# Sixteen-tile Strassen in the head phases, with most new sample states made later

## The chip, the cores and the metric

The kernel runs on one core of one Trainium2 chip. The metric is the device time of one execution in microseconds (us). Before the change it is 2170.14 us, the median of three runs (2167.53 to 2170.44).

## The reference

One inference step of a two-layer decoder trunk, in float32. A prompt group of 512 tokens and a sample group of 8 tokens share all weights, so the kernel works on 520 columns. Cut to what matters:

```python
def trunk_layer(x, p_i, pos, conv_buf, ret_S, norm_g, w_in, conv_w, gn_g, w_out, w_pg, w_ple):
    h = rmsnorm(x, norm_g)
    z = h @ w_in                                   # 2048 -> 8192
    b_c, c_c, x_c, g_c, q, k, v, g_r = split_projection(z)
    conv_y, new_buf = short_conv(c_c * x_c, conv_buf, conv_w)
    y_conv = b_c * conv_y * jax.nn.silu(g_c)
    q = rope(q...); k = rope(k...) * (RET_HEAD_DIM ** -0.5)
    o, new_S = retention(q, k, v, ret_S, retention_log_gamma())
    o = groupnorm(o, per head)
    y_ret = (o * gn_g) * jax.nn.silu(g_r)
    x = x + jnp.concatenate([y_conv, y_ret], axis=-1) @ w_out
    x = x + jax.nn.sigmoid(x @ w_pg) * (p_i @ w_ple)
    return x, new_buf, new_S
```

For a sample token the retention of one head (256 x 256 state S, 4 heads, 8 sample rows, so 32 states per layer) is S_new = gamma S + k v and o = q . S_new, which is also gamma (q . S) + (q . k) v. The new states are an output of the step, and o goes on into the group norm.

## The kernel before, in words

Activations lie transposed: 16 K tiles of 128 features by 520 columns. Every float32 product is made of three matmuls (`mm3`, L245 to L249): operands and weights are split into a high part, written by ACT, and the rest, written by DVE (`split_w`, L229 and L230, for weights; `split`, L551 and L552, for activations).

The projections run in pairs of 128-row output tiles (`pair`). A pair is computed plainly (`plain`) or with its first s K tiles by Strassen's scheme (`strassen`): two rows, two halves of the columns (260 each) and two halves of the K tiles form a 2 x 2 block product of seven products instead of eight. The rest of the K tiles, `chunks(s, KT)`, is done plainly into the same banks, with one more bank, `c`. Weight sums are made by DVE in `add` (L319) in place in the raw ring of 32 tiles; bank copies and sums are L307 and L312. Operand sums (`operand_sums`, L413 to L416) are made once per operand set and split. The number of Strassen tiles per pair stands in tables: `HEADS` and `CONVS` for the input projection, `OUT_ROWS` and `GATES` for the two others.

A layer has these phases. Heads: 16 pairs, four for each retention head (q, k, v, gate), and the prompt's retention in nine steps per head, popped aside of later pairs. Convolution: 8 steps j of two pairs. Then the output projection `wo` (8 pairs), and the gate projection `wg` with the embeddings (8 pairs, in the last layer 7 and an ending of its own). Each phase builds the operand set of the next as room allows (`Operands.fill`, with a reserve).

All buffers for activations are 75 slots of 520 columns, handed out first in, first out (`Slots`); split weights go through a ring of 60 tiles. Weight loads are issued by SP. Everything else, loads and stores of slots, goes through POOL's queue (`SIDE`). A simulated time line orders each engine's instructions by program order as priority; operations passed to `keep` stay in program order among themselves.

Sample states: `sample` is called from `head` (three times per two pairs) and from the convolution steps. It loads a state (`sample_load`: L770, and key and query of that row broadcast to all partitions, L771), and one call later runs `sample_step`: ACT scales the state by gamma (L776), DVE adds k v in two operations (L780), POOL stores the new state (L781), and two reductions (L784) make q . S_new into `osum`. After the last one `sample_norm` (L1371 to L1389) normalises all rows, beside the last convolution step.

Of the kernel before, what the change touches and what calls it, by code (L numbers as in the profile page):

```python
# [7 lines left out]
F32 = mybir.dt.float32  # L8
# [5 lines left out]
P = 128  # L14
D = 2048
KT = D // P
# [10 lines left out]
PLE = 256  # L27
PAST = 4096
EPS = 1e-6
NSLOT = 75  # L30
CH = 4
CHS = 4
CHA = 4
# [28 lines left out]
RAW = 32  # L62
WARM = 8
FIRST = 8
SPLIT = 60


def F(ap):
# [11 lines left out]
class Slots:  # L80
# [111 lines left out]
def trunk_kernel(  # L192
# [365 lines left out]
        return op  # L558


    vec = const.tile([P, 160], F32, name="vec")

    def norm_g(l, k):
        return vec[:, 16 * l + k : 16 * l + k + 1]
# [12 lines left out]
        c = 112 + 4 * h + m  # L577
        return vec[:, c : c + 1]

    def gam(h):  # L580
        return vec[:, 128 + h : 129 + h]
# [6 lines left out]
    scv = const.tile([P, CJ, 2, NS], F32, name="scv")  # L588
    vs = const.tile([P, H, 2, NS], F32, name="vs")
    osum = const.tile([P, 2, H, NS], F32, name="osum")  # L590
    gs = const.tile([P, 2 * H, NS], F32, name="gs")
    decay = const.tile([P, H, 3], F32, name="decay")

    G.memset(ones, 1.0)
    G.memset(onesd, 1.0 / HD)
    G.memset(half_neg, -0.5)

    yc = dram.tile([DEPTH, CJ, P, T], F32, name="yc")
    x1s = dram.tile([DEPTH, KT, P, T], F32, name="x1s")
# [75 lines left out]
    for a, b in ((0, 1), (1, 4), (4, 8), (8, 12), (12, 16)):  # L675
        raws = []
        if b == 1:
            raw = raw_ring.get(4)
            DMA.dma_start(raw.rearrange("p (m n) -> p m n", n=P), wi[0, 0:4, :, :P].rearrange("m p n -> p m n"))
            S.dma_start(vec, vecs)  # L680
            x = get()
            for n in (LEFT, RIGHT):
                DMA.dma_start(x[:, n], xT[0, :, n])
            xs.append(x)
            w = split_w(raw)
            ws = [[t[:, P * m : P * m + P] for t in w] for m in range(4)]
        else:
            for i in range(4):
                raws.append(load(wi[0, i, :, P * a : P * b]))
                if i < b - a:  # L690
                    x = get()
                    DMA.dma_start(x, xT[a + i])
                    xs.append(x)
            ws = [split_w(raw) for raw in raws]
            raw_ring.put(*raws)
        for k in range(a, b):
            X.ops[k] = split(xs[k], norm_g(0, k), free_src=False, halves=k % 2 == 0 and k < max(X.rows))
            for m in range(4):
                for h, n in enumerate((LEFT, RIGHT)):
                    product(first[m][h], ws[m], k - a, at(X.ops, [k], n), k == 0, k == KT - 1)  # L700
        if b == 1:
            raw_ring.put(raw)
            split_ring.put(*w)
            DMA.dma_start(ident, ident_d)
        else:
            for w in ws:
                split_ring.put(*w)
# [8 lines left out]
    for l in range(DEPTH):  # L716
# [49 lines left out]
            return g  # L766

        def sample_load(h, b):
            st, kb = get(), get()
            SIDE.dma_start(st[:, :512], sret[l, h, b])  # L770
            SIDE.dma_start(kb[:, :512], kq[l, h, b].rearrange("c d -> (c d)").partition_broadcast(P))  # L771
            return h, b, st, kb

        def sample_step(h, b, st, kb):

            keep(S.activation(st[:, :512], st[:, :512], AF.Identity, scale=gam(h)))  # L776
            k = kb[:, 256:512]
            for e in range(2):
                c = slice(256 * e, 256 * e + 256)
                keep(V.scalar_tensor_tensor(st[:, c], k, vs[:, h, e, b : b + 1], st[:, c], MUL, ADD))  # L780
            SIDE.dma_start(o_rets[l, h, b], st[:, :512])  # L781
            for e in range(2):
                c = slice(256 * e, 256 * e + 256)
                V.tensor_tensor_reduce(k, st[:, c], kb[:, :256], 1.0, 0.0, MUL, ADD, osum[:, e, h, b : b + 1])  # L784
            put(st, kb)

        loaded = []

        def sample():

# [2 lines left out]
            if todo:  # L793
                loaded.append(sample_load(*todo.pop(0)))

        todo = []

        res = xT if l == 0 else x2s[l - 1]
# [18 lines left out]
        def retain(h):  # L817
# [28 lines left out]
            vf = []  # L846
            for e, z in enumerate(head(mt + 4)):
                t = z.slot if z.ps is None else copied(z.ps).slot
                V.scalar_tensor_tensor(vs[:, h, e, :], t[:, SEQ:T], 1.0 / 16, rb[:, SEQ:T], MUL, MUL)
# [227 lines left out]
        for j in range(CJ):  # L1077
            mt = 32 + 4 * j
            O.ready = min(j // 2, 3)
            middle.append(sample)  # L1080
            zc, zx = pair(X, wi[l], mt, mt // 2 - skipped, O)
            u = get()
            times(u, zc, r2)
# [17 lines left out]
            if j == CJ - 1:  # L1101
                while loaded or todo:
                    sample()
                O.ready = 7
                sample_norm(nc, small, pr, osum, onesd, half_neg, gs, lambda k: gn_g(l, k))
            zg, zb = pair(X, wi[l], mt + 2, mt // 2 + 1 - skipped, O)
            gt = silu(zg)
            V.tensor_tensor(t, t, gt, MUL)
            put(gt)
# [20 lines left out]
        for m in range(0, KT, 2):  # L1130
            xs = [get(), get()]
            for i in range(2):
                SIDE.dma_start(xs[i], res[m + i])
            Gt.ready = m // 2
            middle.append(lambda: O.fill(MORE_OUT, 0))
            zs = pair(O, wo[l], m, m // 2, Gt)
            for i, (x, z) in enumerate(zip(xs, zs)):
# [37 lines left out]
        for m in range(0, KT - tail, 2):  # L1175
            pes, xs = [], [again(x1s, m), again(x1s, m + 1)]
            later.append(lambda m=m, w=parts(wp[l, m // 2], 0, 4), pes=pes: embed(m, w, pes))
            if X:
                X.ready = m // 2
            middle.append(lambda: Gt.fill(MORE_GATE, 0))  # L1180
            if tail and m == KT - tail - 2:
# [33 lines left out]
        if tail:  # L1215
# [141 lines left out]
                    DMA.dma_start(o_ys, few)  # L1357

            block_out(1)
        if l < DEPTH - 1:  # L1360
            X.ready = KT // 2


def sample_norm(nc, small, pr, osum, onesd, half_neg, gs, gn):

    V, G, PE = nc.vector, nc.gpsimd, nc.tensor
    n = H * NS
    flat = osum.rearrange("p e h b -> p e (h b)")
    ps = pr.tile([P, 512], F32, tag="r", name="ps_sm")
    for e in range(2):  # L1370
        PE.matmul(ps[:, :n], onesd, flat[:, e], start=e == 0, stop=e == 1)  # L1371
# [107 lines left out]
```

## Time and profile before

| | before |
|---|---|
| time of three runs, us | 2167.53, 2170.14, 2170.44 |
| span of the profiled execution, us | 2167.3 |
| DMA, mean | 179 GB/s, 387.31 MB |
| matmul records | 17861 |

The span goes from the first to the last instruction of one execution on the core; a run's time holds the span and what lies around it. The profiled execution is one, its own run time isn't listed. PE is TensorE, DVE VectorE, ACT ScalarE, POOL GpSimd, SP the engine that issues the weight loads. PEld is the loading of matmul weights, which overlaps PE. Busy times of PE are modelled, since matmuls are pipelined. In the groups of instructions, the columns are: line, engine, operation, output<-inputs, output shape<-input shape, count, then busy us and mean ns of one, then the idle time of the engine just before them and what released it.

### The profile page before, as it was taken

The page shows a single profiled execution, that of the slowest core. Times are in us where ns is not written, and L with a number is a line of the kernel's source. Part 1 is how long each engine was busy: PE and PEld are TensorE (multiplying, and loading weights), DVE is VectorE, ACT ScalarE, POOL GpSimd, SP SyncE. Part 2 cuts the span into 40 slices and gives each one's busy share as a digit, 9 for nine tenths or more (in the row PEclk, how much of TensorE's full clock was granted, in tenths as well). Part 3 has the DMA queues.
Part 4 walks back from the last instruction along what each step waited for, and adds up shares of the span by engine and source line. Part 5 has one row for each costly group of instructions (what it writes and reads, how often), then busy time and mean ns, then how long its engine had stood idle before and what let it go on. Part 6 is the DMA issues. An engine that isn't in the chain of part 4 may idle for free. (4 is left out here: it accounts for less than half of the span.)

```text
span 2167.3 us, 48178 instructions
## 1 busy us (share of the span) xinstructions
PE 2147.8 (99%) x17861; PEld 2142.1 (99%) x17861; DVE 1896.1 (87%) x3849; ACT 1264.5 (58%) x2647; POOL 430.6 (20%) x746
## 2 busy tenths in 40 slices
PE   9999999999999999999999999999999999999998
PEld 9999999999999999999999999999999999999998
DVE  8889988998999987987997988989999998879884
ACT  8656655565555655655765655565645555456565
POOL 2313222211001211200212222231111022011011
PEclk9999999999999999999999999999999999999999
DMA  8555565545543745645645566664464355566455
GB/s 288 171 175 197 181 217 184 178 157 175 158 129 118 238 156 187 215 154 160 215 144 175 172 213 191 189 209 170 151 182 149 120 158 202 176 207 200 128 164 198
DMA packets 182861, 387.31 MB, mean 179 GB/s; under 512 B 25888, under 2 KB 56352, under 8 KB 182624
## 3 DMA queue, kind: packets, MB, share of 16 engines
q1 hardware_dynamic: 128704, 212.98, 31.6%
q0 software_dynamic: 53056, 169.84, 23.8%
q8 instruction: 140, 2.29, 0.4%
q10 hardware_dynamic: 864, 1.39, 0.2%
q14 instruction: 97, 0.79, 0.1%
HBM read 318.96 MB, written 65.15 MB: 177 GB/s over the span
## 5 line engine op out<-in xcount | busy, mean ns | idle before, releaser
L247 PE MATMUL ps_g<-slot,split 128*128 128x260 f32 x5465 | 1531.6, 284 | 7.2 <-ACT slot L307 2.9
L248 PE MATMUL ps_g<-slot,split 128*128 128x260 f32 x5465 | 1534.3, 282 | 0.3 <-DVE slot L555 0.3
L249 PE MATMUL ps_g<-slot,split 128*128 128x260 f32 x5461 | 1519.9, 283 | 0.5 <-DVE split L230 0.5
L229 ACT ACTIVATE split<-raw 128x512 fp32r<-128x512 f32 (+2 forms) x1347 | 777.3, 596 | 583.1 <-DVE raw L319 213.2
L247 PEld LDWEIGHTS ps_g<-slot,split 128*128 128x128 f32 x5465 | 1024.0, 188 | 10.1 <-ACT slot L307 3.7
L248 PEld LDWEIGHTS ps_g<-slot,split 128*128 128x128 f32 x5465 | 1028.5, 188 | 0.5 <-DVE slot L555 0.5
L249 PEld LDWEIGHTS ps_g<-slot,split 128*128 128x128 f32 x5461 | 1019.8, 188 | 1.0 <-DVE split L230 1.0
L230 DVE TENSOR_TENSOR split<-raw,split 128x512 fp32r<-128x512 f32 (+2 forms) x1346 | 849.2, 652 | 172.5 <-PE ps_g L248 85.4
L319 DVE TENSOR_TENSOR raw<-raw 128x512 f32<-128x512 f32 (+1 forms) x660 | 428.9, 660 | 32.5 <-DMA raw<-wi 23.7
L307 ACT ACTIVATE slot<-ps_g 128x260 f32<-128x260 f32 x336 | 127.4, 381 | 140.6 <-PE ps_g L249 122.7
L551 ACT ACTIVATE slot<-slot 128x520 fp32r<-128x520 f32 (+1 forms) x212 | 109.2, 562 | 46.6 <-DVE slot L414 11.1
L552 DVE TENSOR_TENSOR slot<-slot,slot 128x520 fp32r<-128x520 f32 (+1 forms) x212 | 124.4, 620 | 4.1 <-ACT slot L551 3.9
L781 POOL DMA_DIRECT2D o_rets<-slot x64 | 35.3, 552 | 351.6 <-DVE slot L780 131.7
L307 DVE TENSOR_TENSOR slot<-ps_g,slot 128x260 f32<-128x260 f32 x168 | 70.9, 424 | 6.0 <-PE ps_g L249 3.7
L869 POOL DMA_DIRECT2D slot<-hs x64 | 46.2, 724 | 118.7 <-DVE split L230 42.7
L814 POOL DMA_DIRECT2D hs<-slot x64 | 35.6, 556 | 139.3 <-DVE slot L755 61.3
L780 DVE SCALAR_TENSOR_TENSOR slot<-slot,vs,slot 128x256 f32<-128x256 f32 x128 | 56.1, 481 | 4.5 <-ACT slot L776 4.3
L746 DVE TENSOR_TENSOR slot<-slot,slot 128x520 f32<-128x520 f32 x80 | 55.8, 698 | 4.7 <-DMA o_rets<-slot 3.7
L770 POOL DMA_DIRECT2D slot<-sret x64 | 35.5, 554 | 114.6 <-ACT split L229 37.3
L1058 POOL DMA_DIRECT2D slot<-x1s x76 | 40.8, 538 | 87.6 <-PE ps_g L249 27.2
L1209 POOL DMA_DIRECT2D x2s<-slot x30 | 16.4, 545 | 201.6 <-DVE slot L1204 200.6
L771 POOL DMA_DIRECT2D slot<-kq x64 | 34.9, 547 | 106.0 <-DVE slot L876 22.2
(217 smaller groups left out, 1733.8 us busy)
## 6 DMA issues: line engine op xcount, KB each, us to landing
raw<-wi SPq DMA_DIRECT2D x377, 256.0 KB, 3.9
raw<-wo SPq DMA_DIRECT2D x128, 256.0 KB, 5.4
raw<-wg SPq DMA_DIRECT2D x122, 256.0 KB, 4.1
raw<-wi SPq DMA_DIRECT2D x136, 192.0 KB, 4.0
slot<-x1s POOLq DMA_DIRECT2D x76, 260.0 KB, 5.1
slot<-sret POOLq DMA_DIRECT2D x64, 256.0 KB, 4.0
hs<-slot POOLq DMA_DIRECT2D x64, 256.0 KB, 4.0
slot<-hs POOLq DMA_DIRECT2D x64, 256.0 KB, 5.2
```

Source lines behind the costliest of these rows:

```text
L229: S.activation(hi, raw, AF.Copy)
L230: V.tensor_tensor(lo, raw, F(hi), SUB)
L247: PE.matmul(out, wh, xh, start=start, stop=False, skip_group_check=more)
L248: PE.matmul(out, wh, xl, start=False, stop=False, skip_group_check=more)
L249: PE.matmul(out, wl, xh, start=False, stop=stop, skip_group_check=more)
L307: fn(*args)
L319: V.tensor_tensor(out[:, n], x[:, n], y[:, n], op)
L551: keep(S.activation(hi, src[:, n], AF.Copy))
L552: V.tensor_tensor(lo, src[:, n], F(hi), SUB)
L746: V.tensor_tensor(out[:, n], v, table[:, n], MUL)
L780: keep(V.scalar_tensor_tensor(st[:, c], k, vs[:, h, e, b : b + 1], st[:, c], MUL, ADD))
L869: SIDE.dma_start(t[:, :512].rearrange("p (m n) -> p m n", m=2), src)
```

## The change

Head pairs that had 14 Strassen tiles get 16; so do the first two convolution pairs of each layer. The slots go from 75 to 76, the split ring from 60 to 56 tiles, and the table `vec` from 160 to 128 columns, since gamma becomes a constant of the instruction.

For 24 of the 32 sample states of a layer (rows b below 6) the new state is no longer made in `sample_step`. Only gamma (q . S) is reduced there, from the old state; the queries of two rows share a slot. The term (q . k) v is added in `sample_norm`, from products `qk` summed over the partitions by two matmuls with ones. The new states are made later by `update`, three calls deep: load the key, multiply it by v / gamma (two ACT operations), add the old state by an accumulating load from DRAM, and a call later scale by gamma and store. `update` is called three times per convolution step from the fourth on, once per pair in the output phase (m = 2 to 12) and in the gate phase (m = 2 to 10).

```diff
-NSLOT = 75
+NSLOT = 76
-HEADS = [[0, 0, 0, 8] + [14] * 12, [0] + [14] * 15]
-CONVS = [[14] * 2 + [16] * 13 + [14]] * 2
+GAMMA = [1.0 - 2.0 ** (-5 - h) for h in range(H)]
+HEADS = [[0, 0, 0, 8] + [16] * 12, [0] + [16] * 15]
+CONVS = [[16] * 15 + [14]] * 2
-SPLIT = 60
+SPLIT = 56
+LATE_STATES = 6
+UPDATES = 3
...
         def sample_load(h, b):
-            st, kb = get(), get()
+            st = get()
             SIDE.dma_start(st[:, :512], sret[l, h, b])
-            SIDE.dma_start(kb[:, :512], kq[l, h, b].rearrange("c d -> (c d)").partition_broadcast(P))
-            return h, b, st, kb
+            if b >= LATE_STATES:
+                kb = get()
+                SIDE.dma_start(kb[:, :512], kq[l, h, b].rearrange("c d -> (c d)").partition_broadcast(P))
+                return h, b, st, kb
+            if b % 2 == 0:
+                n = min(2, LATE_STATES - b)
+                queries.append(get())
+                src = kq[l, h, b : b + n, :2].rearrange("b c d -> b (c d)").partition_broadcast(P)
+                SIDE.dma_start(queries[-1][:, : 256 * n].rearrange("p (b c) -> p b c", b=n), src)
+            return h, b, st, queries[-1]
...
         def sample_step(h, b, st, kb):
...
+            for e in range(2):
+                c = slice(256 * e, 256 * e + 256)
+                n = slice(256 * (b % 2), 256 * (b % 2) + 256)
+                keep(V.tensor_tensor_reduce(st[:, c], st[:, c], kb[:, n], GAMMA[h], 0.0, MUL, ADD, osum[:, e, h, b : b + 1]))
+            put(st)
+            if b % 2 or b == LATE_STATES - 1:
+                put(kb)
...
+        def key_load(h, b):
+            st = get()
+            SIDE.dma_start(st[:, 256:512], kq[l, h, b, 2:].rearrange("c d -> (c d)").partition_broadcast(P))
+            return h, b, st
+
+        def state_add(h, b, st):
+            for e in range(2):
+                c = slice(256 * e, 256 * e + 256)
+                keep(S.activation(st[:, c], st[:, 256:512], AF.Copy, scale=vs[:, h, e, b : b + 1]))
+            SIDE.dma_start(st[:, :512], sret[l, h, b], accum_op=ADD)
+            return h, b, st
+
+        def state_out(h, b, st):
+            keep(S.activation(st[:, :512], st[:, :512], AF.Copy, scale=GAMMA[h]))
+            SIDE.dma_start(o_rets[l, h, b], st[:, :512])
+            put(st)
+
+        keyed, added = [], []
+
+        def update():
+            if added:
+                state_out(*added.pop(0))
+            if keyed:
+                added.append(state_add(*keyed.pop(0)))
+            if states:
+                keyed.append(key_load(*states.pop(0)))
+
+        states = [(h, b) for b in range(LATE_STATES) for h in range(H)]
...
+            some = slice(0, LATE_STATES)
+            V.scalar_tensor_tensor(qk[:, :, h, some], qks[:, :2, some], GAMMA[h], qks[:, 2:, some], MUL, MUL)
...
-                V.scalar_tensor_tensor(vs[:, h, e, :], t[:, SEQ:T], 1.0 / 16, rb[:, SEQ:T], MUL, MUL)
+                V.scalar_tensor_tensor(vs[:, h, e, :], t[:, SEQ:T], 1.0 / 16 / GAMMA[h], rb[:, SEQ:T], MUL, MUL)
+                rest = slice(SEQ + LATE_STATES, T)
+                V.scalar_tensor_tensor(vn[:, h, e, :], t[:, rest], 1.0 / 16, rb[:, rest], MUL, MUL)
...
             middle.append(sample)
+            if j >= UPDATES:
+                middle.append(update)
...
             zg, zb = pair(X, wi[l], mt + 2, mt // 2 + 1 - skipped, O)
+            if j >= UPDATES:
+                update()
...
             middle.append(lambda: O.fill(MORE_OUT, 0))
+            if 0 < m < KT - 2:
+                middle.append(update)
             zs = pair(O, wo[l], m, m // 2, Gt)
...
             middle.append(lambda: Gt.fill(MORE_GATE, 0))
+            if 0 < m < KT - 4:
+                middle.append(update)
...
+    ps = pr.tile([P, 512], F32, tag="r", name="ps_qk")
+    for d in range(2):
+        PE.matmul(ps[:, :n], ones, qk[:, d].rearrange("p h b -> p (h b)"), start=d == 0, stop=d == 1)
+    own = small.tile([P, 2, H, NS], F32, tag="sq", name="own", bufs=1)
+    for e in range(2):
+        V.tensor_tensor(own[:, e], vs[:, :, e], ps[:, :n].rearrange("p (h b) -> p h b", b=NS), MUL)
+        V.tensor_tensor(osum[:, e], osum[:, e], own[:, e], ADD)
     ps = pr.tile([P, 512], F32, tag="r", name="ps_sm")
```

The parts left out are the eight early rows of `sample_step` (as before, with gamma as a constant and `vn` for the values), the second `update` of a convolution step ahead of its second pair, and the declarations of `qk`, `vn` and `own`.

More of the change, by code (lines that the diff above doesn't have):

```diff
@@ L558, in split @@
         return op
-    vec = const.tile([P, 160], F32, name="vec")
+    vec = const.tile([P, P], F32, name="vec")
     def norm_g(l, k):
@@ L590, in trunk_kernel @@
     osum = const.tile([P, 2, H, NS], F32, name="osum")
+    qk = const.tile([P, 2, H, NS], F32, name="qk")
+    vn = const.tile([P, H, 2, NS - LATE_STATES], F32, name="vn")
     gs = const.tile([P, 2 * H, NS], F32, name="gs")
@@ L679, in trunk_kernel @@
             DMA.dma_start(raw.rearrange("p (m n) -> p m n", n=P), wi[0, 0:4, :, :P].rearrange("m p n -> p m n"))
-            S.dma_start(vec, vecs)
+            S.dma_start(vec, vecs[:, :P])
             x = get()
@@ new lines, in sample_load @@
+            if b % 2 == 0:
[4 more added lines that the diff above has]
+            return h, b, st, queries[-1]
+        def sample_step(h, b, st, kb):
+            if b >= LATE_STATES:
+                keep(S.activation(st[:, :512], st[:, :512], AF.Copy, scale=GAMMA[h]))
+                k = kb[:, 256:512]
+                for e in range(2):
+                    c = slice(256 * e, 256 * e + 256)
+                    v = vn[:, h, e, b - LATE_STATES : b - LATE_STATES + 1]
+                    keep(V.scalar_tensor_tensor(st[:, c], k, v, st[:, c], MUL, ADD))
+                SIDE.dma_start(o_rets[l, h, b], st[:, :512])
+                for e in range(2):
+                    c = slice(256 * e, 256 * e + 256)
+                    V.tensor_tensor_reduce(k, st[:, c], kb[:, :256], 1.0, 0.0, MUL, ADD, osum[:, e, h, b : b + 1])
+                put(st, kb)
+                return
@@ L778, in sample_step @@
             for e in range(2):
                 c = slice(256 * e, 256 * e + 256)
[L780 to L787, printed above, removed]
+                n = slice(256 * (b % 2), 256 * (b % 2) + 256)
@@ L794, in sample @@
                 loaded.append(sample_load(*todo.pop(0)))
+        def key_load(h, b):
[4 more added lines that the diff above has]
+            for e in range(2):
+                c = slice(256 * e, 256 * e + 256)
+                keep(S.activation(st[:, c], st[:, 256:512], AF.Copy, scale=vs[:, h, e, b : b + 1]))
+            SIDE.dma_start(st[:, :512], sret[l, h, b], accum_op=ADD)
+            return h, b, st
+        def state_out(h, b, st):
+            keep(S.activation(st[:, :512], st[:, :512], AF.Copy, scale=GAMMA[h]))
+            SIDE.dma_start(o_rets[l, h, b], st[:, :512])
+            put(st)
[8 more added lines that the diff above has]
+        states = [(h, b) for b in range(LATE_STATES) for h in range(H)]
         todo = []
@@ L1104, in trunk_kernel @@
                 O.ready = 7
-                sample_norm(nc, small, pr, osum, onesd, half_neg, gs, lambda k: gn_g(l, k))
+                sample_norm(nc, small, pr, osum, qk, vs, ones, onesd, half_neg, gs, lambda k: gn_g(l, k))
+            if j >= UPDATES:
+                middle.append(update)
             zg, zb = pair(X, wi[l], mt + 2, mt // 2 + 1 - skipped, O)
+            if j >= UPDATES:
+                update()
             gt = silu(zg)
@@ L1359, in trunk_kernel, with sample_norm @@
             block_out(1)
+        assert not (todo or loaded or states or keyed or added)
         if l < DEPTH - 1:
             X.ready = KT // 2
-def sample_norm(nc, small, pr, osum, onesd, half_neg, gs, gn):
+def sample_norm(nc, small, pr, osum, qk, vs, ones, onesd, half_neg, gs, gn):
     V, G, PE = nc.vector, nc.gpsimd, nc.tensor
@@ L1368, in sample_norm @@
     flat = osum.rearrange("p e h b -> p e (h b)")
+    ps = pr.tile([P, 512], F32, tag="r", name="ps_qk")
+    for d in range(2):
+        PE.matmul(ps[:, :n], ones, qk[:, d].rearrange("p h b -> p (h b)"), start=d == 0, stop=d == 1)
+    own = small.tile([P, 2, H, NS], F32, tag="sq", name="own", bufs=1)
+    for e in range(2):
+        V.tensor_tensor(own[:, e], vs[:, :, e], ps[:, :n].rearrange("p (h b) -> p h b", b=NS), MUL)
+        V.tensor_tensor(osum[:, e], osum[:, e], own[:, e], ADD)
     ps = pr.tile([P, 512], F32, tag="r", name="ps_sm")
```

10 lines of the change are left out of this document (6 added, 4 removed).

## The prediction

> **What bounds the kernel now.** I read the head of the page first (busy time by engine, then the 40 slices), after it the table of stages, the matmul groups with shapes kept apart, and the waits of PE.
>
> ```profile
> span 2167.3 us, 48178 instructions
> ...
> PE 2147.8 (99%) x17861; PEld 2142.1 (99%) x17861; DVE 1896.1 (87%) x3849; ACT 1264.5 (58%) x2647; POOL 430.6 (20%) x746
> ...
> PEclk9999999999999999999999999999999999999999
> ```
>
> ```profile
> core 0: us, PE busy (x) PEld busy (x) DVE busy (x) ACT busy (x) POOL busy (x), PEclk, DMA share, GB/s
> 0.00:100.00 100.00, 97.24 (x777) 95.85 (x778) 83.20 (x162) 70.23 (x140) 29.99 (x61) 1.00 0.68 231
> 100.00:600.00 500.00, 499.06 (x4170) 498.81 (x4169) 453.44 (x969) 291.59 (x627) 112.58 (x193) 1.00 0.57 180
> 600.00:800.00 200.00, 196.68 (x1636) 196.05 (x1635) 180.82 (x356) 112.97 (x244) 32.70 (x51) 1.00 0.53 164
> 800.00:1000.00 200.00, 200.00 (x1671) 200.00 (x1670) 169.38 (x314) 112.11 (x215) 30.10 (x56) 1.00 0.56 179
> 1000.00:1600.00 600.00, 598.93 (x5000) 597.74 (x4999) 534.97 (x1140) 362.64 (x775) 140.78 (x239) 1.00 0.58 183
> 1600.00:1800.00 200.00, 197.72 (x1640) 196.46 (x1639) 185.46 (x371) 113.30 (x244) 26.32 (x39) 1.00 0.50 156
> ...
> 2000.00:2167.30 167.30, 158.17 (x1313) 157.22 (x1311) 119.37 (x234) 92.14 (x197) 22.71 (x41) 0.99 0.50 163
> ```
>
> ```profile
> L247 PE MATMUL ps_g<-slot,split 128*128 128x260 f32 x5437 | 1523.6, 284 | 7.2 <-ACT slot L307 2.9 <-ACT ps_g L307 1.6 <-ACT split L229 1.5
> ```
>
> PE sets the time, at the full granted clock: it is idle for 2167.3 - 2147.8 = 19.5 us. By the table, 2.8 of these lie in the first 100 us, 9.1 in the last 167, 3.3 + 2.3 in the two stretches where the convolution phase hands over to the output projection (600:800 and 1600:1800), and 0.9 + 1.1 in all the rest. A matmul's mean of 284 ns is its pipelined length; its price is the distance between starts. In 800:1000, where PE never waits, 1671 starts fill 200 us: **0.1197 us each**. Nearly all of them are the 260-column matmuls, so a matmul taken away is worth 0.12 us as long as weights, operands and bank copies still come in time.
>
> **What the change removes.** A pair of output tiles costs 16 x 2 x 2 x 3 = 192 matmuls when plain. With s K tiles by Strassen it costs 7 x (s/2) x 3 plus (16 - s) x 4 x 3, which is 192 - 1.5 s: 171 for s = 14 and 168 for s = 16. From 14 to 16 go 12 head pairs of layer 0, 15 of layer 1, and two convolution pairs in each layer (the last one stays at 14): 31 pairs, 93 matmuls. **93 x 0.1197 = 11.1 us less on PE.**
>
> **What it adds on PE.** sample_norm gets two more matmuls of 32 columns per layer, beside two of that shape:
>
> ```profile
> 664.56 0.28 PE L249 MATMUL ps_g<-slot,split 128*128 128x260 f32 x1
> 664.68 0.53 PE L1371 MATMUL ps_sm<-osum,onesd 128*128 128x32 f32 x4
> 665.04 0.36 PE L247 MATMUL ps_g<-slot,split 128*128 128x260 f32 x1
> 665.24 0.28 PE L248 MATMUL ps_g<-slot,split 128*128 128x260 f32 x1
> ```
>
> The two of before hold the stream up by 665.24 - 664.68 - 0.12 = 0.44 us. Two more in two layers: **+0.9 us**. The four small DVE operations behind them (the nearest row is L849's 165 ns, below) delay the sample gates by under 1 us; those feed operands of the next phase and no matmul at once, so I put nothing down.
>
> **What a 16-tile pair costs the others.** DVE stands at 453.44 / 500 = 91% in the heads, so it must not grow.
>
> ```profile
> L230 DVE TENSOR_TENSOR split<-raw,split 128x512 fp32r<-128x512 f32 x1031 | 695.0, 690 | 147.8 <-PE ps_g L248 81.2 <-ACT split L229 51.8 <-issue 6.1
> L319 DVE TENSOR_TENSOR raw<-raw 128x512 f32<-128x512 f32 x520 | 354.1, 688 | 17.6 <-DMA raw<-wi 12.1 <-DMA raw<-wo 2.9
> L230 DVE TENSOR_TENSOR split<-raw,split 128x384 fp32r<-128x384 f32 x249 | 137.1, 555 | 16.2 <-ACT split L229 9.9 <-PE ps_g L248 3.4 <-ACT slot L551 1.9
> ...
> L319 DVE TENSOR_TENSOR raw<-raw 128x384 f32<-128x384 f32 x140 | 77.4, 554 | 14.9 <-DMA raw<-wi 11.6 <-DMA raw<-wg 2.8
> ...
> L780 DVE SCALAR_TENSOR_TENSOR slot<-slot,vs,slot 128x256 f32<-128x256 f32 x128 | 56.1, 481 | 4.5 <-ACT slot L776 4.3
> ...
> L230 DVE TENSOR_TENSOR split<-raw,split 128x256 fp32r<-128x256 f32 x66 | 27.3, 423 | 8.5 <-ACT split L229 7.6 <-PE ps_g L248 0.8
> ...
> L849 DVE SCALAR_TENSOR_TENSOR vs<-slot,slot 128x8 f32<-128x8 f32 x16 | 2.5, 165 | 0.1
> ```
>
> Splits per pair: 14 of 512 columns (9.66 us) for 7 of 512, 7 of 384 and 2 of 256 (9.56 us). The four weight sums grow by 4 x (688 - 554) ns = 0.54 us. Together +0.64 us. Against it, each late state drops its two L780 operations, 0.96 us. The heads take about 1.5 samples per pair and three in four are late: -1.08 us. New values and the q.k products add some 0.14 us per pair (L849's 165 ns twice and one like it, per head of four pairs). Net -0.3 us per 20 us pair: DVE keeps its margin. The price of that cover being gone: DVE at 18.2 us of work per 20 us pair has 1.8 us to spare, so +0.64 us without relief, as in the first head, is still hidden. SP issues 8 weight loads per pair where it issued 10, of the same bytes; the raw ring of 32 tiles is then full with four matrices of 8, as it is now in 13 convolution pairs per layer and in all 16-tile output pairs, which run at 200.00 of 200.
>
> The split ring loses 4 of 60 tiles: 7 chunks in flight instead of 7.5, that is 7 x 12 x 0.12 = 10 us of lead. PE does not feel half a chunk as long as ACT is the one that waits:
>
> ```profile
> ACT split L229 <- PE ps_g L249: 186.2, 220, 3.9
> ```
>
> It does, 220 times. I cost it at nothing; a hiccup of over 10 us would be needed.
>
> **Operands.** A 16-tile pair needs the eighth operand sum at once. Does it exist by then?
>
> ```profile
> L416 DVE TENSOR_TENSOR slot<-slot,slot x8: 421/430/435, 41.3 to 95.5; 128x260 f32<-128x260 f32 x8
> ```
>
> ```profile
> 1103.21 0.43 DVE L416 TENSOR_TENSOR slot<-slot,slot 128x260 f32<-128x260 f32 x1
> ...
> 1114.41 0.70 DVE L552 TENSOR_TENSOR slot<-slot,slot 128x520 fp32r<-128x520 f32 x1
> ```
>
> In layer 0 all eight sums (one L416 each) are made by 95.5 us, and the first pair concerned starts after 384 + 192 + 180 = 756 matmuls, near 93 us: free. In layer 1 the eighth is summed at 1103.2 and its splits run to 1115, in a stretch where DVE has little spare. One split of 0.70 us becomes due earlier. Bounds: nothing (other work moves back) and 3.1 us (a whole sum: four operations of 0.43 and two splits of 0.70). I take **+0.7 us**.
>
> **Late states.** Each late state keeps its two reductions, and moves elsewhere: a key load, two ACT copies of 256 columns, an accumulating load of the old state, one ACT copy of 512, the store.
>
> ```profile
> L229 ACT ACTIVATE split<-raw 128x512 fp32r<-128x512 f32 x1032 | 632.3, 626 | 462.3 <-DVE raw L319 188.2 <-PE ps_g L249 166.4 <-PE ps_g L248 45.1
> ...
> L776 ACT ACTIVATE slot<-slot,vec 128x512 f32<-128x512 f32 x64 | 45.7, 714 | 0.0
> ...
> L917 ACT ACTIVATE slot<-ps_kt,vec 128x256 fp32r<-128x256 f32 x32 | 15.0, 468 | 9.2 <-DMA hs<-slot 3.2 <-DVE slot L918 2.5 <-PE ps_kt L913 2.2
> ```
>
> ```profile
> L770 POOL DMA_DIRECT2D slot<-sret x64: 537/544/585, 50.5 to 1670.9; - x64
> ```
>
> ```profile
> slot<-sret POOLq DMA_DIRECT2D x64, 256.0 KB, 4.0
> ...
> slot<-kq POOLq DMA_DIRECT2D x64, 256.0 KB, 4.8
> o_rets<-slot POOLq DMA_DIRECT2D x64, 256.0 KB, 3.1
> ```
>
> ACT: 2 x 0.47 + 0.63 - 0.71 = +0.86 us per late state, at most three states per 40 us in the convolution phase and one per 20 us later, on an engine busy 55 to 60% there. POOL: 4.5 DMA issues for 3, so 48 x 1.5 x 0.54 = 39 us on an engine at 20%. Bytes: a second read of 48 x 256 KB = 12.6 MB. None of it feeds a matmul: **0** on PE, if nothing queues behind a wait. Queued behind an ACT wait are the weight splits; behind a POOL wait, the operand loads. No row has an accumulating load. The nearest are the plain load of that state, 4.0 us, as the low end, and twice that, 8.0 us, as the high end, since it reads its target too. Emitted steps lie half a pair (10 us) or more apart, so either fits; I take 4.0 us.
>
> **Slots.** Two more are held through the output and gate phases and one is added. I count 76 of 76 in use in the gate phase (64 operands, 4 of the embeddings, 1 of the norm, 2 rows, 2 results, 1 square, 2 states); 74 of 75 before. Loads there have a whole pair until use: 0, range -1 to +3 us at the phase borders.
>
> **Sum.** -11.1 + 0.9 + 0.7 = **-9.5 us** on the span: 2157.8. The three runs had 2167.5 to 2170.4, the median 2170.14 being 2.8 above the profiled span. With the same 2.8: **2160.6 us**. The case's own range is 2157 to 2165.
>
> **Rivals.** *PE waits at the borders take the gain* (18%). For: nearly all idle time inside the run is at borders (3.3 + 2.3 us), where DVE is full and ACT's copies come late. Two slots fewer for operands built ahead could double it, with another 2 to 3 us at the start of layer 1: 2160.6 + 5.6 + 2.5 = 2168.7. Against: a rough count of free slots shows the first operand pair of the output phase delayed by one product only, about 3 us, before it is late.
>
> *The accumulating load lands later than the order assumes, and ACT stands in front of it* (12%): the slower side. Place: the convolution phase from its fourth step, 15 states per layer, DVE at 185.46 / 200 = 93%. If each of 30 copies waits d, the splits behind it slip by d, and 400 us of this phase have 7%, 29 us, to catch up. It decides from d = 1 us; at d = 2 us it costs 60 - 29 = 31 us: 2191. Against: ACT's L776 sat 0.0 us idle for 64 plain loads of the same states. [...]
>
> *More than counted* (8%): with fewer L780 in the heads, some of the 2 us of PE waits there and part of the borders' go too: 2155 to 2157.
>
> *The forecast* has 62%. About 0.2% (4.3 us) is what a measurement of this kernel can tell from no change; so faster 0.70, same 0.18, slower 0.12. The range 2156.5 to 2171 holds the forecast, the borders' case and a little of the gain beyond: about 0.8.
>
> **What would show it.** PE busy near 2138 and 93 fewer 260-column matmuls, at the same 0.1197 us; no L319 of 384 columns outside the pairs that stay at 14 or below; ACT without a long idle time ahead of the copy that leads to the late store; the 600:800 and 1600:1800 stretches with no more idle PE than 3.3 and 2.3 us. I am wrong if PE's waits grow by over 5 us: at the borders (slots), or ahead of splits in the late convolution steps (the accumulating load).

## The result, and the profile after

After the change the kernel takes 2208.93 us (median of four runs, 2205.45 to 2210.52), before it 2170.29 in the same session: a ratio of 1.0176 with a 95% interval of 1.0161 to 1.019. It is slower by 38.6 us, where 9.5 less were forecast; the time lies outside the range.

The head of the page of after (busy time by engine):

```profile
span 2208.7 us, 47858 instructions
...
PE 2158.7 (98%) x17776; PEld 2144.5 (97%) x17776; DVE 1885.8 (85%) x3723; ACT 1287.8 (58%) x2650; POOL 495.9 (22%) x819
```

The table of stages of after, with the columns of the one of before:

```profile
0.00:100.00 100.00, 95.92 (x764) 94.84 (x765) 81.05 (x158) 68.43 (x135) 28.72 (x61) 0.98 0.67 227
100.00:600.00 500.00, 496.17 (x4117) 495.06 (x4117) 446.11 (x908) 278.19 (x572) 106.52 (x173) 0.99 0.53 167
600.00:800.00 200.00, 185.01 (x1487) 180.67 (x1486) 166.66 (x332) 118.68 (x261) 52.55 (x79) 0.99 0.62 180
800.00:1000.00 200.00, 200.00 (x1670) 200.00 (x1669) 166.74 (x308) 118.72 (x235) 45.14 (x78) 1.00 0.65 203
1000.00:1600.00 600.00, 595.11 (x4929) 592.19 (x4929) 532.69 (x1072) 348.65 (x707) 127.60 (x209) 1.00 0.53 171
1600.00:1875.00 275.00, 264.37 (x2149) 261.17 (x2148) 235.76 (x471) 159.79 (x346) 64.28 (x97) 0.99 0.61 180
...
2000.00:2208.70 208.70, 197.18 (x1634) 195.78 (x1632) 153.73 (x302) 120.32 (x251) 36.49 (x63) 0.98 0.55 176
```

The matmuls went: each of the three lines that hold the 260-column matmuls has 31 records fewer (5406 for 5437), 93 together as counted, and eight small ones of `ps_qk` are new, 85 fewer in all. A start still costs 0.1197 us (1670 in the 200 us of 800:1000). PE is idle for 2208.7 - 2158.7 = 50.0 us where it was 19.5. A sharper measure is the **lost time** of a stretch, its length less its starts times 0.1197 us; it holds idle time and whatever else delays a start. For the stretches of the table, after against before: 100:600 7.2 against 0.9; 600:800 22.0 against 4.2; 1000:1600 10.0 against 1.5; 1600:1875 17.8 against 3.7 (before: 1600:1800). Over the whole span it is 2208.7 - 17776 x 0.1197 = 80.9 against 2167.3 - 17861 x 0.1197 = 29.3: 51.6 us more are lost, 85 x 0.1197 = 10.2 are saved, and the span is 41.4 longer.

The waits of ACT and DVE in after (who waits for whom: us in total, times, longest) and PE's largest group with what ended its idle time:

```profile
ACT split L233 <- PE ps_g L252: 401.2, 405, 4.5
DVE split L234 <- ACT split L233: 187.9, 229, 4.6
```

```profile
L251 PE MATMUL ps_g<-slot,split 128*128 128x260 f32 x5406 | 1519.4, 285 | 31.3 <-ACT split L233 19.7 <-ACT slot L311 5.5 <-ACT slot L558 1.7
L831 ACT ACTIVATE slot<-slot 128x512 f32<-128x512 f32 x48 | 29.9, 623 | 27.9 <-DMA slot<-sret 27.9
```

PE waits for ACT's splits (19.7 us; 1.5 before). Two things stand in ACT's row of work: the wait for a free place in the split ring, and L831, the late state's copy ahead of its store, which waits 27.9 us for the accumulating load.

### The profile page after: what moved, and what is told of

Read it like the earlier page. It is cut to its first block, busy times and chain, and to the rows that moved or that the text cites. A ratio compares the mean times of both kernels' runs of the same rounds, so it can differ in the third digit from the quotient of the medians.

```text
span 2208.7 us, 47858 instructions
## 1 busy us (share of the span) xinstructions
PE 2158.7 (98%) x17776; PEld 2144.5 (97%) x17776; DVE 1885.8 (85%) x3723; ACT 1287.8 (58%) x2650; POOL 495.9 (22%) x819
## 5 line engine op out<-in xcount | busy, mean ns | idle before, releaser
L251 PE MATMUL ps_g<-slot,split 128*128 128x260 f32 x5434 | 1527.4, 285 | 31.3 <-ACT split L233 19.7
L233 ACT ACTIVATE split<-raw 128x512 fp32r<-128x512 f32 (+1 forms) x1285 | 785.8, 626 | 711.9 <-PE ps_g L252 401.2
L234 DVE TENSOR_TENSOR split<-raw,split 128x512 fp32r<-128x512 f32 (+1 forms) x1284 | 856.8, 686 | 198.0 <-ACT split L233 187.9
L323 DVE TENSOR_TENSOR raw<-raw 128x512 f32<-128x512 f32 (+1 forms) x660 | 445.8, 686 | 43.4 <-DMA raw<-wi 31.4
L311 ACT ACTIVATE slot<-ps_g 128x260 f32<-128x260 f32 x336 | 124.7, 373 | 44.9 <-PE ps_g L253 41.4
L924 POOL DMA_DIRECT2D slot<-hs x64 | 46.3, 724 | 183.0 <-DVE osum L804 37.5
L774 POOL DMA_DIRECT2D slot<-sret x64 | 36.0, 562 | 182.3 <-ACT split L233 41.0
L832 POOL DMA_DIRECT2D o_rets<-slot x48 | 26.4, 550 | 138.5 <-ACT slot L831 134.8
L827 POOL DMA_DIRECT2D slot<-sret x48 | 42.7, 889 | 33.6 <-ACT slot L826 22.2
L826 ACT ACTIVATE slot<-slot,vs 128x256 f32<-128x256 f32 x96 | 47.9, 499 | 0.3
```

Source lines behind the costliest of these rows:

```text
L233: S.activation(hi, raw, AF.Copy)
L234: V.tensor_tensor(lo, raw, F(hi), SUB)
L251: PE.matmul(out, wh, xh, start=start, stop=False, skip_group_check=more)
L311: fn(*args)
L323: V.tensor_tensor(out[:, n], x[:, n], y[:, n], op)
L826: keep(S.activation(st[:, c], st[:, 256:512], AF.Copy, scale=vs[:, h, e, b : b + 1]))
```

## Experiments

Ratios are to the kernel before, measured beside each, with 95% intervals.

### The parts alone

*heads16_only*: before with the new tables and nothing else.

```diff
-HEADS = [[0, 0, 0, 8] + [14] * 12, [0] + [14] * 15]
-CONVS = [[14] * 2 + [16] * 13 + [14]] * 2
+HEADS = [[0, 0, 0, 8] + [16] * 12, [0] + [16] * 15]
+CONVS = [[16] * 15 + [14]] * 2
```

> The kernel before with the 16-tile tables alone; 75 slots, split ring of 60, sample states as before. Theory L (the late states cost the time): the 93 matmuls go and nothing else, 2170 - 11 = 2159 us. Rival H (16-tile head pairs, with the raw ring full, starve the splits): about 2200 us, with PE waiting for splits in the heads. Rival R (the shorter split ring): 2159 us here too, since the ring is not shortened.

Measured: 2186.15 us, 1.0073 [1.0049, 1.0097]. Rows of its table of stages:

```profile
100.00:600.00 500.00, 490.10 (x4052) 487.76 (x4051) 454.35 (x928) 284.57 (x580) 114.94 (x194) 0.99 0.56 178
600.00:800.00 200.00, 197.76 (x1637) 196.42 (x1637) 184.65 (x364) 112.63 (x242) 31.72 (x49) 1.00 0.52 162
1000.00:1600.00 600.00, 588.91 (x4872) 585.95 (x4871) 539.59 (x1087) 353.86 (x717) 139.29 (x236) 0.99 0.57 180
```

Lost are 500 - 4052 x 0.1197 = 15.0 us and 600 - 4872 x 0.1197 = 16.8 us, in the heads, where before lost 0.9 and 1.5. Without late states the 16-tile heads cost more than their matmuls save. None of the times expected (2159 or about 2200) was met.

*heads16_ring56*: the same with `SPLIT = 56`, `NSLOT = 76` and 132 columns of `vec` to make room.

> As heads16_only, but with 76 slots and the split ring of 56 tiles, so everything of the change except the late states. Theory L: 2159 to 2161 us. Rival H: about 2200 us. Rival R (ring of 56): above heads16_only by 10 us or more, most of it where DVE is full.

Measured: 2215.91 us, 1.0214 [1.0194, 1.0234]: 29.8 us above heads16_only, as rival R of the shorter ring had it.

*late_states_only*: the change with the old tables.

```diff
-HEADS = [[0, 0, 0, 8] + [16] * 12, [0] + [16] * 15]
-CONVS = [[16] * 15 + [14]] * 2
+HEADS = [[0, 0, 0, 8] + [14] * 12, [0] + [14] * 15]
+CONVS = [[14] * 2 + [16] * 13 + [14]] * 2
```

> The change with the head and convolution tables put back to 14; late states, 76 slots and ring of 56 stay. Theory L: the matmuls come back and the waits stay, 2209 + 10 = 2219 us, with PE waits at the end of the convolution phase. Rival H: about 2171 us. Rival R: 2185 us or more.

Measured: 2215.35 us, 1.0212 [1.0192, 1.0231], 6.4 us above the change, which theories L and R both allowed: with late states in place the new tables cost nothing, and may save some of their matmuls' time, though a new order alone can make such a difference (below). The loss is in the rest.

### The split ring

*ring56_only*: before with `SPLIT = 56`. *change_ring60*: the change with `SPLIT = 60` and `NSLOT = 75`. *change_ring52*: the change with `SPLIT = 52`.

```diff
-SPLIT = 60
+SPLIT = 56
```

> The kernel before with the split ring cut from 60 to 56 tiles and nothing else. Theory P (parity: with an even number of 4-tile groups each high part takes the place of a high part, so ACT waits for the same chunk of matmuls as DVE and DVE then waits for ACT; with 15 groups high and low swap places and ACT runs ahead): DVE's wait on ACT rises from 69 us, 2175 to 2195 us, since the phases with 16 tiles pay and the heads with their 3-tile chunks less. Theory D (only the depth counts, half a chunk of seven): 2169 to 2172 us.

> The change with the ring of 60 tiles as before and 75 slots for room. Theory P and theory D both: faster than the change by the 30 us that the ring cost the 16-tile heads, about 2180 us, with the late convolution steps still stalling behind the accumulating load. If the late states alone were the cost: above 2200 us.

> The change with a split ring of 52 tiles (13 groups, odd, but shallower than its 56). Theory P: faster than the change although the ring is shorter, DVE's wait on ACT falls from 188 us to under 100, 2180 to 2192 us. Theory D: slower than the change, 2212 us or more.

Measured: ring56_only 2188.4 us, 1.0106 [1.0091, 1.0121]; change_ring60 2186.09, 1.0089 [1.0074, 1.0104]; change_ring52 2207.84, 1.0195 [1.0177, 1.0212]. Four tiles are worth 21.5 us in the kernel before (2166.88 beside it, the same slots), 29.8 with 16-tile heads, and in the change 22.8, or 18.9 by the ratios, as the two were not timed together (in these two pairs the version with 60 tiles has 75 slots instead of 76). PE's own waits say the same: what it stands for splits, all such rows of its waits added up, rises from 2.5 to 9.4 us in the first pair, from 10.7 to 19.9 in the second and from 9.7 to 23.9 in the third. In change_ring60:

```profile
100.00:600.00 500.00, 499.82 (x4187) 499.61 (x4186) 456.67 (x926) 286.26 (x588) 108.87 (x177) 1.00 0.53 169
600.00:800.00 200.00, 190.45 (x1538) 187.69 (x1537) 168.02 (x333) 117.16 (x261) 58.94 (x79) 0.98 0.62 188
1000.00:1600.00 600.00, 598.01 (x4990) 596.89 (x4989) 541.37 (x1096) 352.56 (x716) 131.85 (x218) 1.00 0.54 175
1600.00:1875.00 275.00, 263.82 (x2150) 261.85 (x2150) 233.71 (x456) 160.06 (x348) 69.45 (x96) 0.98 0.60 180
```

The heads lose -1.2 and 2.7 us instead of 7.2 and 10.0 (4187 starts in 500 us are 0.1194 us each, so the measure is good to about 1 us): they run as they did before, with 16 tiles and relief. The late stretches of the convolution still lose 15.9 and 17.6.

Why should four tiles matter? Counted in chunks of 4, a ring of 60 shared by high and low parts in turn has 15 places: high part n reuses the place of low part n - 8, low part n that of high part n - 7, so ACT may be 8 chunks ahead of PE and DVE 7. With 14 places both wait for chunk n - 7, ACT first and DVE behind it. The waits of ring56_only show that, and its time is the one expected from it:

```profile
ACT split L229 <- PE ps_g L248: 346.9, 384, 3.9
DVE split L230 <- ACT split L229: 175.3, 217, 4.6
```

Before, DVE's wait for ACT was 69.3 us in 77 times. The first theory was that this serial wait is the cost; the rivals were too few tiles and, later, the shortest lead. *ring56_swapped* exchanges the two parts' places in every second chunk of ring56_only:

```diff
+        turn[0] += 1
+        if turn[0] % 2:
+            hi, lo = lo, hi
```

> ring56_only (2188 us) with the two halves of every second chunk exchanged, so that with 14 groups, too, a high part takes the place of a low part: the same depth, the order of places as with an odd number. Theory P1 (what matters is whose place the high part takes): DVE's wait on ACT falls from 175 us to under 100, 2167 to 2175 us. Theory P2 (what matters is that with 15 groups ACT may write eight chunks ahead while DVE's part is seven ahead; the exchange gives ACT no such lead): the wait stays above 150 us, 2184 to 2192 us.

Measured: 2200.19 us, 1.0147 [1.013, 1.0165], with DVE's wait for ACT at 183.0 us. The place isn't it: the wait stays as long as both leads are equal. (The time is above the 2184 to 2192 us that went with this theory.) change_ring52 speaks against the serial wait itself: its 13 places give leads of 7 and 6, DVE's wait for ACT falls from 187.9 to 81.2 us as that theory had it, and the time stays at that of the change, where 2180 to 2192 us were expected. The next four give high and low parts rings of their own in the kernel before:

```diff
-    split_ring = Ring(const, SPLIT, F32R, "split")
+    split_ring = TwoRings(Ring(const, 32, F32R, "split_hi"), Ring(const, 24, F32R, "split_lo"))
```

> The kernel before with its ring of split weights cut into two of their own: 32 tiles for high parts (8 chunks of 4) and 24 for low parts (6 chunks), 56 tiles together, as in the change. Theory of the serial wait: what costs is that ACT and DVE wait for the same chunk to be freed. Here ACT may be 8 chunks ahead and DVE 6, so ACT's part is done before DVE's place comes free: DVE waits for PE and not for ACT (DVE's split behind ACT's: below 90 us of idle time), and the time is within 0.4% of before. Rival, the number of tiles: 56 tiles, and 6 chunks for the low parts, are less lead than 7, so the time is that of the shared ring of 56 (+1.0%) or more.

> The kernel before with two rings of 28 tiles for high and low parts, 7 chunks each. Theory of the serial wait: both engines wait for the same chunk, as in the shared ring of 56: +0.8 to +1.5%, DVE's split behind ACT's for about 175 us. Rival, that a shared ring hands out awkward places (parts of 384 or 256 columns split it up): rings of their own are free of that, and the time is near before.

> The kernel before with rings of their own: 32 tiles for high parts (8 chunks of 4) and 28 for low parts (7 chunks), 60 tiles together, the leads that the shared ring of 60 gives. Theory of the lead (how many chunks ACT and DVE may be ahead of PE sets what PE loses): as before, ratio 0.997 to 1.004, since ring_28_and_28 differs from it by ACT's eighth chunk alone and took 17.5 us more. Rival, that two rings change the order and this alone costs: 1.005 to 1.01.

> The kernel before with two rings of 30 tiles, 60 together: seven whole chunks of 4 tiles each and two tiles over. Theory of the lead: both engines may be 7 whole chunks ahead, as with 28 and 28, so ratio 1.005 to 1.01 in spite of 60 tiles. Rival, the number of tiles: as before (1.0 within 0.3%), since Strassen's parts of 3 and 2 tiles use the tiles that are over.

| rings | leads of ACT, DVE (chunks) | DVE waits for ACT, us | PE waits for splits, us | ratio |
|---|---|---|---|---|
| 60 shared (before) | 8, 7 | 69.3 | 2.5 | 1 |
| 32 and 28 | 8, 7 | 74.8 | 6.6 | 1.0056 [1.0039, 1.0072] |
| 30 and 30 | 7, 7 | 176.4 | 7.5 | 1.0071 [1.0056, 1.0086] |
| 28 and 28 | 7, 7 | 187.2 | 7.8 | 1.0082 [1.0067, 1.0098] |
| 56 shared | 7, 7 | 175.3 | 9.4 | 1.0106 [1.0091, 1.0121] |
| 32 and 24 | 8, 6 | 83.7 | 22.5 | 1.0247 [1.0232, 1.0261] |

The waits of ring_32_and_24:

```profile
ACT split_hi L242 <- PE ps_g L261: 229.5, 221, 5.3
DVE split_lo L243 <- PE ps_g L262: 118.3, 122, 3.7
DVE split_lo L243 <- ACT split_hi L242: 83.7, 79, 4.6
```

The serial wait appears exactly where the leads are equal, so the count of places is right; but it is **not what sets the time**: 32 and 24 is without it and the slowest by far, and 32 and 28 is without it and still 0.56% slower than before. The number of tiles alone isn't it either (30 and 30 has 60). 32 and 24 met its rival, 28 and 28 and 30 and 30 the theories for equal leads. What goes with the time, row by row, is how long PE stands for splits. The time rises as the shortest lead falls, 7 to 6, which speaks for the lead; against it stand change_ring52, whose low parts have a lead of 6 and which is no slower than 56 (2207.84 against 2208.93), and 32 and 28, which has the leads of before and met its rival's 1.005 to 1.01. What remains of the rows is partly a new order, as the next two show.

### What any new order costs

*gamma_constant*: gamma as a constant of L776 in the kernel before, 64 instructions of the same shape, each 0.09 us shorter (0.62 for 0.71). *one_warm_matmul_less*: `WARM = 7` for 8.

```diff
-            keep(S.activation(st[:, :512], st[:, :512], AF.Identity, scale=gam(h)))
+            keep(S.activation(st[:, :512], st[:, :512], AF.Copy, scale=1.0 - 2.0 ** (-5 - h)))
```

> The kernel before with gamma as a constant of ACT's scale and nothing else: a neutral edit of 64 operations that gives the scheduler a slightly different order. Theory N (any new order loses what the old one had, whatever the edit): 2180 us or more. Theories P and L: 2166 to 2172 us.

> The kernel before with 7 instead of 8 warming matmuls at its start: a second neutral edit, which shifts the scheduler's clock by a fraction of a microsecond. Theory N (a new order costs about 10 us whatever the edit): 2172 to 2180 us. Otherwise 2166 to 2169 us.

Measured: 2177.2 us, 1.0045 [1.003, 1.0061], and 2169.38, 1.0004 [0.9995, 1.0014]. An edit that adds no work moved the time by 10 us, to between its two forecasts, another by nothing. Differences of up to some 10 us between two versions can't be put down to a mechanism by the time alone; the ring's 19 to 30, in three pairs and with PE's waits for splits rising in each, can (gamma_constant has 4.1 us of these waits, ring56_only 9.4).

### The late states

*late_no_accumulate*: the accumulating load as a plain one (it overwrites k v, so the late states lack that part).

```diff
-            SIDE.dma_start(st[:, :512], sret[l, h, b], accum_op=ADD)
+            SIDE.dma_start(st[:, :512], sret[l, h, b])
```

> The change with the accumulating load of the old state replaced by a plain load of it (the k v term of the late new states is left out). Theory L1 (the accumulating load lands some 2 to 3 us later than the order of ACT assumes): ACT's wait ahead of the late scale falls from 28 us to under 5 us and the time to about 2180 us. Theory L2 (where the late steps stand and what they queue up with on POOL and in the DMA engines is the cost, however the state is loaded): stays above 2200 us.

Measured: 2191.72 us, 1.0104 [1.0088, 1.0121], 17.2 us below the change (15.6 by the ratios). Neither forecast was met: ACT's wait falls by half and not to under 5 us, since a plain load in this place takes 5.8 us to land where the accumulating one takes 6.6. The wait that ended ACT's idle time ahead of L831, and two rows of its table of stages:

```profile
ACT slot L831 <- DMA slot<-sret: 14.5, 10, 3.4
```

```profile
600.00:800.00 200.00, 194.18 (x1575) 192.30 (x1574) 175.06 (x345) 122.46 (x269) 49.83 (x82) 0.98 0.60 191
...
1600.00:1875.00 275.00, 269.57 (x2213) 268.18 (x2212) 241.10 (x473) 166.33 (x359) 60.73 (x101) 0.99 0.59 188
```

11.5 and 10.1 us are lost there where the change lost 22.0 and 17.8: 18.2 less in the two stretches, about all of what the run gained. In the change's own trace (the queries by line and the timeline):

```profile
L827 POOL DMA_DIRECT2D slot<-sret x48: 868/884/927, 547.7 to 2103.4; - x48
...
DMA to landing us min/median/max: 4.0/6.6/9.7
```

```profile
651.58 0.87 POOL L827 DMA_DIRECT2D slot<-sret  x1 [1.34 <-ACT slot L826]
...
653.96 0.64 ACT L233 ACTIVATE split<-raw 128x512 fp32r<-128x512 f32 x1 [0.32 <-PE ps_g L252]
657.40 0.63 ACT L831 ACTIVATE slot<-slot 128x512 f32<-128x512 f32 x1 [2.80 <-DMA slot<-sret]
...
659.00 0.39 PE L251 MATMUL ps_g<-slot,split 128*128 128x260 f32 x1 [0.67 <-ACT split L233]
```

The load of this state was issued at 651.58, ACT reached its copy at 654.60, and it landed 5.8 us after its issue. The splits queued behind the copy followed at 658.34, and PE stood for one until 659.00. Issue and use were 3 us apart, not 10. So it is in all ten waits of L831, one in each convolution step from the fourth on: ACT reached the copy 2.2 to 4.6 us after the issue, and the copy could start 4.1 to 8.8 us after it. The other 38 copies waited for nothing.

*add_in_dram*: change_ring60, where the heads scale the old state by gamma on ACT and store it, and late steps add k v to it by an accumulating store in DRAM, so ACT waits for no load there, and the second read and the second scale fall away (the diff is cut to the late step).

```diff
-            SIDE.dma_start(st[:, :512], sret[l, h, b], accum_op=ADD)
-            return h, b, st
+            SIDE.dma_start(o_rets[l, h, b], st[:, :512], accum_op=ADD)
+            put(st)
```

> The change with the ring of 60 and 75 slots (change_ring60, 2186 us), and the late states made another way: the head phase scales the old state by gamma and stores it, the late step stores k v onto it with an accumulating store into DRAM, so that ACT waits for no accumulating transfer and the second read and the second scale fall away. Theory L1 (ACT's waits for the accumulating load): ACT's 20 us of waits are gone, the convolution stretches lose under 5 us of PE each instead of 10 and 11, 2168 to 2174 us. Theory L2 (place and traffic of the late steps): 2182 us or more.

Measured: 2177.25 us, 1.0041 [1.0028, 1.0055], against 1.0089 of change_ring60, between the two forecasts and no more than a new order can make. ACT's waits are gone, and yet PE idles 8.5 and 7.1 us in the two convolution stretches (9.6 and 11.2 in change_ring60). The traces of these two runs show another wait, which no other run has at this length: DVE's for a POOL operation of `sample_norm`, the same 10.7 us in both, here from change_ring60:

```profile
DVE dl L1460 <- POOL rsn L1458: 10.7, 2, 5.4
```

It comes once per layer, beside the last convolution step; the operation takes 12.6 to 13.4 us there and 5.8 in before. In the 30 us around it PE idles for 4.8 and 4.0 us in change_ring60 and 3.9 and 3.7 in add_in_dram, mostly for DVE's splits. Whether the late steps or the order alone brought the operation there, no run tells. *no_late_in_conv*: change_ring60 with 16 late states per layer for 24, none made beside the convolution, and a second one in the output pairs.

```diff
-LATE_STATES = 6
-UPDATES = 3
-TWICE = ()
+LATE_STATES = 4
+UPDATES = 8
+TWICE = (0, 2, 4, 6, 8, 10, 12)
```

> The change with the ring of 60 and 75 slots, 16 instead of 24 late states per layer and none of their steps in the convolution phase (one or two per pair of the output phase, one per pair of the gate phase). Theory L1 or L2 (the late convolution steps are where they hurt): PE idle in the two convolution stretches falls from 9.6 and 11.2 us to under 5 each; part comes back in the heads, where DVE has less relief; 2172 to 2182 us. If the place is not the point: 2186 us or more with the idle time still in those stretches.

Measured: 2179.13 us, 1.005 [1.003, 1.0071]. Its table of stages:

```profile
600.00:800.00 200.00, 198.29 (x1640) 196.89 (x1639) 177.93 (x349) 115.23 (x251) 40.60 (x61) 1.00 0.57 173
...
1600.00:1875.00 275.00, 272.44 (x2265) 271.61 (x2264) 245.83 (x477) 156.76 (x331) 46.13 (x70) 1.00 0.52 163
```

3.7 and 3.9 us are lost there, as before, and the forecast was met. So with the late steps the loss of these stretches goes, too: 33.5 us together in change_ring60, 7.6 without these steps. That holds DVE's wait above as well, which this run doesn't have. Most of the gain is lost again elsewhere: PE is idle for 6.7 us in 800:1100 and 5.2 in 1875:2150, where the late steps now are; before had 0.0 and 1.1 there.

*dram_add_after_conv* joins the two, the add in DRAM and the three constants above; *dram_add_late_conv* is that with `LATE_STATES = 5` and `UPDATES = 7`.

> The version with the add in DRAM (ring of 60, 75 slots, 16-tile heads), with 16 late states per layer in place of 24, and made only in the output and gate phases, none beside the convolution steps. Theory: what was left over before (8.5 and 7.0 us of idle PE in 600:800 and 1600:1875) comes from late steps beside the convolution, as the version without them had 1.7 and 2.6; and its own 7 and 5 us in the output and gate phases came from ACT's wait for the accumulating load, which this one doesn't have. So idle PE of about 20 us in all and a time 0 to 10 us below before (ratio 0.995 to 1.0). Rival, any change of the order costs some 10 us by shifted work at the borders: ratio 1.003 to 1.006.

> The version with the add in DRAM after the convolution, with 20 late states per layer in place of 16, the first ones beside the last convolution step. Theory: heads lose less PE time (2.4 and 3.8 us more than before in 100:600 and 1200:1650 with 16 late states, 0 with 24), the convolution's last stretch some 2 us more: ratio 0.999 to 1.003. Rival, the losses are a matter of order and not of DVE's relief in the heads: 1.003 to 1.006 as with 16 and with 24.

Measured: 2176.26 us, 1.0032 [1.0021, 1.0043], and 2188.87, 1.0087 [1.007, 1.0103]. The first has the lowest median of the versions with 16-tile heads (add_in_dram is within its interval) and is still slower than before, as its rival had it: in its profiled execution, the fastest of its ten, PE idles 26.7 us, 7.2 more than before, and this and 4.5 us of other delays of starts take up the 10.2 us of matmuls. The second, meant to relieve DVE further, lost 12.6 us to the first and missed both of its forecasts. No version tried beats the kernel before.

## Why the prediction was wrong, point by point

- **The matmuls: right.** 93 were to go and 93 went, at the same 0.1197 us. That 85 records at this price are the forecast 10.2 us as well is luck: the eight small ones were priced at 0.9 us from another row.
- **The split ring: the step that failed.** "PE does not feel half a chunk as long as ACT is the one that waits: [...] I cost it at nothing; a hiccup of over 10 us would be needed." It cost 18.9 to 22.8 us in the change and 21.5 alone. ACT's 220 waits for PE were read as spare lead. They say only that the ring is full, that is, that the ring sets the lead; how much lead PE needs is not in them. With 56 tiles PE stood for splits 23.9 us in the change where it stood 9.7 with 60. Which property of the ring does it (shortest lead, equal leads, order) stays open: serial waiting was shown not to be enough.
- **Late states at 0 on PE: the second failure.** The median landing of 6.6 us (4.0 to 9.7) fits the bounds of 4.0 to 8.0 set for it, but not the 4.0 taken, which came from plain loads in another place; in this place a plain load takes 5.8. What was wrong is "Emitted steps lie half a pair (10 us) or more apart, so either fits": in the ten waits issue and use were 2.2 to 4.6 us apart. The rival named this mechanism, ACT standing in front of the load with splits behind it, and its place. Of its price (30 copies at d each, deciding from 1 us) ten copies waited, 2.8 us each, and PE paid 16 to 17 us for the accumulating load over a plain one, though DVE's slack was said to take up 29. What the late steps cost beyond that is not told apart from the order. The high end, twice the plain load, was the author's estimate from the 4.0 us; twice the plain load in the same place would be 11.6, and 6.6 were measured.
- **Heads' DVE net -0.3 us per pair: right in size.** DVE's share in 100:600 was 90.7% before; with 18.2 - 0.3 = 17.9 us per pair of 20 x 168 / 171 = 19.65 us it should be 91%, and change_ring60 has 456.67 / 500 = 91.3%. But "+0.64 us without relief [...] is still hidden" was wrong: heads16_only lost 29 us more than before in the heads, some 1.1 us for each of 27 pairs. The full raw ring is not the reason, as change_ring60 has it too and loses nothing there.
- **Slots at 0 and operands at +0.7: not told apart.** In the 50 us from 1100 on, where the eighth sum of layer 1 falls, PE idles 1.2 us against 0.4 before, with the shorter ring in it. No run changed the slots alone by one at a given ring; heads16_only and change_ring60 do with 75.
- **Borders (a rival):** the loss at 600:800 and 1600:1800 is there, 32 us more than before by lost time in the rows above. 18 of them went with the accumulating load at the same number of slots; for the rest, late steps, their slots and the shorter ring were not told apart.
- **The sum.** 2208.93 is 48.3 us above the forecast of 2160.6. The ring back at 60 leaves 2186.09, the add moved to DRAM 2177.25. The last 16.7 us stay open; a new order alone moved the kernel before by up to 10. (The 2.8 us from span to time are 1.0 too many: in a run that has both, they are 2208.7 and 2210.52.)

## What to carry to other kernels

When a producer waits for a consumer at a full ring, that isn't proof that the ring is larger than needed (ACT waited 220 times here, and four tiles were worth 21.5 us): take a tile off it by itself and time it before giving the room away, above all where another engine is as full as DVE was in the heads (90.7%). A DMA that ends in a compute engine's wait belongs a whole landing time ahead of that engine's use as the engine's real queue reaches it, not as the steps are emitted (6.6 us in the median here, where ACT reached ten copies 2.2 to 4.6 us after the issue); letting the DMA end in memory took the wait away here, for a gain of 9 us at most. And measure what a neutral edit does before explaining differences of that size.

## What the hardware showed

**A gap in PE's work cost more than its length here.** Idle times of PE in after, from its timeline (start, length and, in brackets, the idle time before):

```profile
345.12 0.39 PE L251 MATMUL ps_g<-slot,split 128*128 128x260 f32 x1 [2.04 <-ACT split L233]
346.37 0.58 PE L251 MATMUL ps_g<-slot,split 128*128 128x260 f32 x1 [0.74 <-ACT slot L311]
...
746.61 0.39 PE L251 MATMUL ps_g<-slot,split 128*128 128x260 f32 x1 [3.03 <-ACT split L233]
```

What follows the first two, in windows of 2.5 us:

```profile
345.00:347.50 2.50, 1.64 (x7) 1.43 (x8) 2.41 (x6) 1.73 (x7) 0.54 (x1) 0.61 0.81 276
347.50:350.00 2.50, 2.50 (x13) 2.50 (x13) 2.50 (x7) 1.32 (x5) 0.47 (x1) 0.50 0.88 320
350.00:352.50 2.50, 2.50 (x14) 2.50 (x13) 0.68 (x3) 0.63 (x1) 1.96 (x5) 0.53 0.54 174
352.50:355.00 2.50, 2.50 (x23) 2.50 (x22) 2.50 (x5) 1.70 (x4) 0.00 (x0) 1.00 0.00 0
```

The granted clock falls to 0.50 at 345.5, between the two gaps, and is back after 6.8 us. Two windows have 13 and 14 matmuls where the one at full clock has 23 (each counts those that reach into it, too), so these two alone lose about 2.3 us to slow matmuls ((23 - 13 + 23 - 14) x 0.1197). Over the span the mean granted clock is 0.993 against 0.999 before: 0.006 x 2208.7 = 13 us, of 51.6 lost; 30.5 are idle time, the rest isn't accounted for. The gap of 2.04 us was followed by the fall, while the 3.03 us ahead of 746.61 left the clock at 1.00 up to 760.

In after the granted clock fell four times between 100 and 2170 us, from 1.00 to 0.50: at 345.53, 768.78, 1437.79 and 1830.32, for 6.83, 3.41, 3.41 and 6.83 us. All its changes in the trace of this run lie whole multiples of 3.41 us apart. In the 3.41 us that end at each of the four falls PE idled for 2.04, 2.18, 2.12 and 2.10 us. With the run cut into stretches of that length from the same points on, it idled for 1.72 us at most in any other of them between 100 and 2170. The gap of 3.03 us lies in two of these stretches, with 1.31 us ahead of 744.89 and 1.72 behind it. Four falls of one run are too few for a limit or a cause.

**An accumulating load into a slot** of 256 KB took POOL 0.884 us to issue and 6.6 us to land (L827 in after). The plain load in its place took 0.548 and 5.8 (late_no_accumulate), the plain loads of the state in the heads of before 0.544 and 4.0. So the addition goes with 0.8 us of the landing, and the place with 1.8.
